# A two-layer diffusion step: one list order through layer 0, and the last output tiles, the norm and the modulation by halves of the tokens

## The chip, the cores and the metric

The kernel runs on one core of a Trainium2 chip, as one program and one launch. The metric is the time of one execution on the device in microseconds (us), the median over runs. The engines are named as in the profile: PE (TensorE matmul), PEld (its weight load), DVE (VectorE), ACT (ScalarE), POOL (GpSimd), SP (SyncE, which issues most DMAs here).

## The reference, cut to what matters

There are 128 prompt tokens and 512 sample tokens of width 1024. The kernel keeps them as 640 columns: two halves of 320, each with 64 prompt and 256 sample tokens. Layer 0 has a convolution branch, layer 1 a state-space branch.

```python
for i in range(DEPTH):                                   # two layers
    hp = rms_norm(yp, norm_g[i]) * (1.0 + sc_p) + sh_p   # shift, scale, gate: silu(cond) @ ada_w
    hs = rms_norm(ys, norm_g[i]) * (1.0 + sc_s) + sh_s
    # layer 0, conformer_branch:
    a, a_gate, z = split(h @ w_in + b_in, 3)             # 3 x 2048 channels
    v = depthwise_conv(a * sigmoid(a_gate), w_dw, b_dw)  # 31 taps; sample tokens in rows of 64
    v = silu(layer_norm(v, ln_g, ln_b))                  # over 2048 channels of a token
    out = (v * silu(z)) @ w_out
    # layer 1, ssd_branch: projection, 5-tap convolution, scan in chunks, norm, w_out
    yp = yp + gt_p * out_p
    ys = ys + gt_s * out_s
```

## The kernel before, in words

Everything lies with channels on the 128 partitions and the 640 tokens along the free axis. A product with a weight tile of 1024 x 128 is made in three passes on PE (high part by high part, high by low, low by high), in two halves of 320 columns: 8 x 3 x 2 = 48 matmuls of 128x320. So each weight tile is loaded (`wf`), rounded by ACT to a high part (`wh`, L477 or L78), and its rest becomes the low part `wl`. In the first part of layer 0 (`split`, L474 to L482) ACT writes minus `wh` into `wl`, and a DMA issued by POOL adds the weight to it from memory. In the rest of layer 0 (`split_w`, L73 to L80) POOL or DVE subtracts.

Layer 0 has 48 such tiles of `w_in`: `a0` to `a15`, `g0` to `g15` (the gate of `a`) and `z0` to `z15`. From an `a` and a `g` tile DVE makes the convolution's input `v` (L529). Of the 31 taps of a channel tile, ACT makes one into an accumulator `cva` in PSUM (L627), DVE adds most of the others there (L635), and `NPOOL[i]` of them are made by ACT (`tp`, L666) and added by POOL to a copy of the sum in SBUF (`cv`, L707). Two accumulators are at work at a time, those of channel tiles `i` and `i + 1`. When `cv[i]` is complete, ACT squares it, and PE sums the tile and its square over the channels (`quarter_sums`, L190: eight matmuls of 160 columns, each of which shows as two in the trace). For tiles 0 to 9 these sums go to spare columns of the PSUM tile of a later `a` product, and DVE adds them to `ssum` in SBUF (L539).

The order of the work on each engine is written out in two ways:

- From the fourth tile of layer 0 (`a1`) to `z6` a list scheduler, the class `Order`, gives it. Chains of steps (Python generators) say which engine a step needs, its duration as planned, what it waits for (`key`, or a free buffer, `get`) and what it frees (`put`). `run` emits the step that can begin first by the plan's clocks; on a tie the lower number of `PRIO0` wins. `PLAN0` is the order of the products on PE. Each engine then works strictly in the order that was emitted; semaphores keep it right whatever the times are.
- From `z7` to layer 1's third tile the code is plain (L742 to L892), in an order that another scheduler makes: the products `z7` to `z15`, the sums of tiles 10 to 15 (into a PSUM tile `pst`), mean and root (L785 to L801), 16 times `normalise` and `gate_z` (L806 to L817), then the output product in three passes over channel tiles m = 0, 1; 2 to 5; 6, 7 (`dense`, L148), where DVE adds each result to the residual `x` (L168) and ACT squares it (L853). Then come the last four blocks of the modulation weights (`ada`), the sum of squares, root and spread (`rps`, `rq`), the modulation to `h_hi` and `h_lo`, and layer 1's first three tiles `dt`, `xs`, `xs`, whose halves are 384 and 256 columns (`ODD`).

From layer 1's fourth tile on a second `Order` with its own priorities plans the rest (`project`, L1006, and so on).

The PSUM tiles: `mm` is two of 2 x 512 columns, `cva` two of 1024. An accumulator is columns 0 to 639 of a `cva` tile.

Of the kernel before, what the change touches and what calls it, by code (L numbers as in the profile page):

```python
# [7 lines left out]
F32 = mybir.dt.float32  # L8
# [29 lines left out]
NCST0 = _n - NCST  # L38


@with_exitstack
def trunk(ctx: ExitStack, tc: tile.TileContext, a: dict):
# [99 lines left out]
    ODD = ((0, 384, 0), (384, NT, 128))  # L142
# [92 lines left out]
    PE, ACT, VE, PO, SP, VL = range(6)  # L235

    class Order:
        def __init__(self, prio):
            self.clock = [0.0] * 5
            self.table = None  # L240
            self.port = 0.0
            self.keys = {}
            self.rings = {}
            self.chains = []
            self.count = 0
            self.prio = prio
            self.same = [-OVER[e_] for e_ in range(5)]

# [46 lines left out]
        def run(self, until=None):  # L295
            while self.chains:
# [4 lines left out]
                for ch in self.chains:  # L301
# [3 lines left out]
                    for n, (eng, dur, fn, table) in enumerate(ways):  # L305
                        shared = eng in (PO, VL)
                        eng = VE if eng == VL else eng
# [96 lines left out]
    with tc.tile_pool(name="l0", bufs=1) as lp:  # L404

        def cs(name, dt=F32):
            return lp.tile([P, NT], dt, tag="cs", bufs=32, name=name)

        ssum = lp.tile([P, 2, QN], F32, name="ssum")
        LAG = 10  # L410
        N_Z = 7

        Z_END = list(range(N_Z, 16))
        order = [32 + j for j in Z_END]

        def z_more(n):
            for _ in range(min(n, len(Z_END))):
                z_tile(Z_END.pop(0))
        ahead = []

        def in_tile(mt):
            while len(ahead) < 2 and order:
                m = order.pop(0)
                ahead.append((m, split_w(a["w_in1"][m], 1024, G)))
            m, (wh, wl) = ahead.pop(0)
            assert m == mt
            ps = mm(f"u{mt}_")
            dense_all(ps, wh, wl, h, [k * 128 for k in range(KD)])
            return ps

# [11 lines left out]
        def rows(t):  # L442
            return t.rearrange("p (r w) -> p r w", w=64)

        sz = [None] * 16

        def z_tile(j):
            ps = in_tile(32 + j)
            sz[j] = cs(f"sz{j}")
            S.activation(out=halves(sz[j]), in_=ps[:, :, 0:HN], func=AF.Silu, bias=c("b_in", 32 + j))  # L450

        def cst_w(name):
            return cs(name)
# [12 lines left out]

        def weights():
            for m in tiles0 + order[:2]:
                yield get("wf")
                wf = gp.tile([P, 1024], F32, tag="wf", bufs=2, name="wf")  # L470
                t = yield op(SP, 0.35, lambda: nc.sync.dma_start(out=wf, in_=a["w_in1"][m]))
                start(split(m, wf), t)

        def split(m, wf):  # L474
            yield get("wh")
            wh = gp.tile([P, 1024], F32R, tag="wh", bufs=3, name="wh")
            t = yield op(ACT, 1.05, lambda: S.copy(out=wh, in_=wf))  # L477
            put("wf", t)
            yield get("wl")
            wl = gp.tile([P, 1024], F32R, tag="wl", bufs=3, name="wl")  # L480
            yield op(ACT, 1.05, lambda: S.activation(out=wl, in_=wh.bitcast(F32), func=AF.Copy, scale=-1.0))  # L481
            t = yield op(PO, 1.1, lambda: G.dma_start(out=wl, in_=a["w_in1"][m], accum_op=ALU.add))  # L482
            t += 4.0
            W0[m] = wh, wl
            post(("w", m), t)
            if m in order[:2]:
                ahead.append((m, W0[m]))

        def product(m, lead=None):
# [3 lines left out]
            if lead is not None:  # L493
                yield op(PE, 1.4, lambda: lead(ps))
            wh, wl = W0[m]
# [12 lines left out]

        def after_g(i, ps, n=None):
# [5 lines left out]
            if n is not None:  # L515
                l, b, ws = rows_[n][0]
                r = ap.tile([P, P], F32, tag="ada_row", bufs=2, name="ada_row")
                t = yield op(ACT, 0.26, lambda: S.copy(out=r, in_=ps[:, 0, HN : HN + 128]))
                rows_[n] = l, b, r
                post(("row", n), t)  # L520
# [3 lines left out]
        def after_a(i, ps, n=None, j=None):  # L524
# [12 lines left out]
            if j is not None:  # L537
                sums = ps[:, :, HN : HN + QN]
# [1306 lines left out]
```

## Time and profile before

| | |
|---|---|
| median of 3 runs | 1101.43 us (1100.14 to 1103.24) |
| the profiled execution's own time | 1099.79 us |
| its span, first to last instruction | 1098.0 us |
| mean granted TensorE clock | 0.989 |
| PE busy | 1055.7 us (96%) |
| DVE busy | 817.2 us (74%) |
| ACT busy | 625.8 us (57%) |
| POOL busy | 467.6 us (43%) |

Busy time is the time in which an engine had an instruction at work; matmuls overlap, so a busy PE can still be one whose clock is halved. In lists of instructions the columns are start and duration in us, engine, line, operation, output<-inputs, shapes, and in brackets the idle time ahead and what ended it. In a table by stretches each engine has its busy time and, in brackets, its instructions.

### The profile page before, as it was taken

Reading aid. Unit: us, or ns where it says so; the run is one execution under the profiler, and the core shown is the slowest. Engines: PE = TensorE matmul, PEld = TensorE weight load, DVE = VectorE, ACT = ScalarE, POOL = GpSimd, SP = SyncE. Lnnn points to the kernel's source line nnn. Section 1 sums busy time; section 2 is a strip of 40 time slices with the busy share of each in tenths; the row PEclk is TensorE's granted clock in tenths of the full one; section 3 lists DMA queues with packets and bytes.
Section 4 is the critical chain, followed back from the end, with each engine's and each line's share of the span. In section 5 each row is a group of like instructions: output and inputs, shape, how many; then the busy total and the mean of one; then the engine's idle time right before and its main releaser. Section 6 shows DMA issues by size and latency. Waiting matters only on the chain.

```text
span 1098.0 us, 19890 instructions
## 1 busy us (share of the span) xinstructions
PE 1055.7 (96%) x7896; PEld 979.0 (89%) x7896; DVE 817.2 (74%) x1155; ACT 625.8 (57%) x1059; POOL 467.6 (43%) x448
## 2 busy tenths in 40 slices
PE   6989999999998999999999999999999999999996
PEld 4889999999988998999899888899889888978896
DVE  2489999999989389413369789988766786767673
ACT  6656777768875366312376657593545473743442
POOL 1128887757998237200000066414551443244313
PEclk9999999999998999999999999999999999999998
DMA  9588788876565111613302463424342414343102
GB/s 361 196 230 204 166 208 203 200 176 145 123 136 114 58 39 41 209 58 118 115 27 91 105 151 104 107 70 125 106 109 84 116 61 113 108 120 94 46 20 96
DMA packets 84526, 135.93 MB, mean 124 GB/s; under 512 B 26705, under 2 KB 49617, under 8 KB 84433
## 3 DMA queue, kind: packets, MB, share of 16 engines
q1 hardware_dynamic: 78240, 113.92, 34.5%
q0 software_dynamic: 5472, 19.93, 10.7%
q8 instruction: 62, 1.02, 0.4%
q10 hardware_dynamic: 720, 0.82, 0.2%
q14 instruction: 32, 0.25, 0.1%
HBM read 129.72 MB, written 4.92 MB: 123 GB/s over the span
## 4 chain that ended last, share of the span: by engine, by line
PE 65%; DVE 19%; ACT 5%; POOL 4%; issue 4%; DMA 2%; SPq 0%; POOLq 0%; DVEq 0%; ACTq 0%
PE pz L1006 8%; PE o L1006 8%; DVE cva L635 7%; PE xs L1006 6%; POOL cv L707 3%; PE o L1515 3%; PE po L1287 2%; PE pst L1224 2%; PE B L1006 2%; PE py L1355 2%; DVE xs L1048 2%; DVE cn L807 2%; PE C L1006 1%; PE o__5617 L148 1%; PE o__5618 L148 1%
## 5 line engine op out<-in xcount | busy, mean ns | idle before, releaser
L635 DVE SCALAR_TENSOR_TENSOR cva<-v,cst,cva 128x540 f32<-128x540 f32 (+12 forms) x359 | 278.0, 821 | 10.2 <-ACT cva L627 5.2
L707 POOL TENSOR_TENSOR cv<-cv,tp 128x490 f32<-128x490 f32 (+5 forms) x121 | 149.7, 1237 | 8.2
L968 ACT CAST wh<-wf 128x1024 fp32r<-128x1024 f32 x53 | 55.5, 1047 | 83.3 <-PE xs L1006 21.1
L666 ACT ACTIVATE tp<-v,cst 128x490 f32<-128x490 f32 (+5 forms) x121 | 82.9, 715 | 31.6 <-POOL cv L707 31.5
L972 DVE TENSOR_TENSOR wl<-wf,wh 128x1024 fp32r<-128x1024 f32 x51 | 67.5, 1323 | 33.3 <-ACT wh L968 32.8
L1006 PE MATMUL o<-yhl,wh 128*128 128x320 f32 x384 | 92.2, 327 | 0.0
L78 ACT CAST wh<-wf 128x1024 fp32r<-128x1024 f32 (+1 forms) x37 | 31.8, 860 | 96.2 <-PE o__5148 L148 38.9
L1006 PE MATMUL pz<-h_hi,wh 128*128 128x384 f32 (+1 forms) x256 | 84.7, 331 | 0.5 <-ACT up L1035 0.5
L1006 PE MATMUL pz<-h_hi,wl 128*128 128x384 f32 (+1 forms) x256 | 79.2, 309 | 0.0
L1006 PE MATMUL pz<-h_lo,wh 128*128 128x384 f32 (+1 forms) x256 | 79.2, 309 | 0.0
L1293 POOL TENSOR_TENSOR y<-y,yo 128x512 f32<-128x512 f32 x32 | 44.6, 1394 | 80.6 <-DVE yo L1291 80.5
L80 DVE TENSOR_TENSOR wl<-wf,wh 128x512 fp32r<-128x512 f32 (+1 forms) x25 | 27.1, 1086 | 68.7 <-ACT wh L78 68.5
L1006 PE MATMUL xs<-h_hi,wh 128*128 128x384 f32 (+1 forms) x224 | 77.5, 346 | 0.0
L1006 PEld LDWEIGHTS o<-yhl,wh 128*128 128x128 f32 x384 | 63.9, 188 | 7.8 <-issue 7.8
L1048 DVE SCALAR_TENSOR_TENSOR xs<-up,cst,xs 128x642 f32<-128x642 f32 x64 | 68.1, 1066 | 2.2 <-ACT xs L1046 0.8
L1006 PE MATMUL xs<-h_hi,wl 128*128 128x384 f32 (+1 forms) x224 | 69.3, 309 | 0.0
L1006 PE MATMUL xs<-h_lo,wh 128*128 128x384 f32 (+1 forms) x224 | 69.2, 309 | 0.0
L1006 PE MATMUL o<-yhl,wl 128*128 128x320 f32 x192 | 59.4, 309 | 0.0
L1168 ACT ACTIVATE gf<-gf,cols 128x128 f32<-128x128 f32 x160 | 49.8, 391 | 16.3 <-DVE gf L1164 16.2
L1162 POOL TENSOR_TENSOR gb<-gb,cols 128x512 f32<-128x512 f32 x20 | 25.5, 1274 | 77.5 <-DMA gb<-acd 77.5
L482 POOL DMA_DIRECT2D wl<-w_in x38 | 33.2, 873 | 53.3 <-ACT wl L481 33.7
L80 POOL TENSOR_TENSOR wl<-wf,wh 128x1024 fp32r<-128x1024 f32 (+1 forms) x12 | 26.4, 2203 | 64.3 <-ACT wh L78 64.3
(764 smaller groups left out, 3491.0 us busy)
## 6 DMA issues: line engine op xcount, KB each, us to landing
wf<-w_in SPq DMA_DIRECT2D x48, 512.0 KB, 3.8
wl<-w_in POOLq DMA_DIRECT2D x38, 512.0 KB, 6.6
wa<-w_ada SPq DMA_DIRECT2D x64, 256.0 KB, 6.5
wf<-w_out SPq DMA_DIRECT2D x24, 512.0 KB, 3.8
wf<-w_xbc SPq DMA_DIRECT2D x24, 512.0 KB, 3.8
gf<-acd SPq DMA_DIRECT2D x40, 256.0 KB, 5.2
wa<-w_ada SPq DMA_DIRECT2D x16, 512.0 KB, 9.9
wf<-w_z SPq DMA_DIRECT2D x16, 512.0 KB, 4.0
```

The source lines that it names most:

```text
L80: sub.tensor_sub(out=wl[:, :n], in0=wf[:, :n], in1=wh[:, :n].bitcast(F32))
L482: t = yield op(PO, 1.1, lambda: G.dma_start(out=wl, in_=a["w_in1"][m], accum_op=ALU.add))
L635: t = yield op(VE, 0.24 + 0.01 * (hi - lo), lambda: V.scalar_tensor_tensor(out=rows64(accs[i], lo, hi), in0=rows64(vs[i], lo + d, hi + d), ...
L666: t = yield op(ACT, 0.72, lambda: S.activation(out=tp[:, :, 0 : hi - lo], in_=rows64(vs[i], lo + d, hi + d), func=AF.Copy, scale=w_dw(i, t ...
L707: t = yield op(PO, 1.12 if i < 14 else 1.3, lambda: G.tensor_add(out=rows64(cv[i], lo, hi), in0=rows64(cv[i], lo, hi), in1=sgs["tp", i, n] ...
L968: S.copy(out=cell["wh"], in_=cell["wf"])
L972: e_.tensor_sub(out=cell["wl"], in0=cell["wf"], in1=cell["wh"].bitcast(F32))
L1006: T.matmul(ps[:, b, at_ : at_ + t1 - t0], lhsT=w_, rhs=t_[:, t0:t1], start=k == 0 and n == 0, stop=k == nk - 1 and n == 2)
L1048: t = yield op(VL, 0.89, lambda: V.scalar_tensor_tensor(out=acc, in0=u[:, d : d + PW], scalar=c("w_c", j * 5 + d), in1=acc, op0=ALU.mult, ...
L1168: t = yield op(ACT, 0.39, lambda: S.activation(out=gv[:, h_, :], in_=gv[:, h_, :], func=AF.Exp, bias=cols1[ch][:, o8 + h_ : o8 + h_ + 1]), ...
L1293: t = yield op(PO, 1.29, lambda: G.tensor_add(out=y, in0=y, in1=yo))
L1515: T.matmul(ps, lhsT=wt, rhs=t_[:, tok], start=k == 0 and n == 0, stop=k == 3 and n == 2)
```

## The change

- `PLAN0` now runs through `z15`, and the list scheduler goes on to the end of layer 1's third tile: statistics, normalisation, output passes, norm, modulation and the three tiles are chains in it. The plain code is gone.
- The weights of the output product and of layer 1's first tiles go through the same chain `split`. Output weights come in 16 tiles of 1024 columns in place of 8 x 512, 8 x 1024 and 8 x 512, and get `wl` by the accumulating DMA; the very first tile and layer 1's three get it by a subtraction on DVE or POOL.
- The sums of all 16 tiles go to columns 640 to 799 of the two `cva` tiles (`whole`), whose columns 0 to 639 are the accumulators, and are added up there by PE; `ssum` in SBUF and its additions are gone, and so is the separate `pst`.
- Mean and root stay in PSUM after they are spread; the four copies to SBUF are gone. The gating product and `y_lo` go to DVE or POOL, whichever the plan finds free first.
- All 16 blocks of modulation weights go ahead of `g` and `z` products (12 before).
- The output tiles m = 6, 7 are made for one half of the tokens, then for the other; residual, squares, root, modulation and layer 1's first three products follow by halves. One of the four weight tiles of that pass lies in buffers of `v`.
- Layer 1 uses halves of 320 everywhere (`EVEN`); steps that read its PSUM tiles are cut accordingly.
- `PRIO0`, `NPOOL` and several planned durations have other values.

The diff, cut to its core:

```diff
+PLAN0 = "a1 g2 g3 a2 g4 a3 g5 a4 g6 a5 a6 g7 g8 z0 a7 a8 g9 g10 a9 a10 g11 g12 a11 z1 a12 g13 a13 z2 z3 z4 g14 g15 a14 z5 a15 z6 z7 z8 z9 z10 z11 z12 z13 z14 z15"
+NPOOL = (11, 8, 15, 11, 6, 10, 12, 5, 3, 9, 2, 2, 5, 8, 7, 6)
...
-        LAG = 10
-        N_Z = 7
...
+            src = [(("w", m), a["w_in1"][m]) for m in tiles0]
+            for pi, nc_ in ((0, 4), (1, 8), (2, 4)):
+                src += [(("out", pi, n), a[f"w_out1_{pi}"][n]) for n in range(nc_)]
+            src += [(("l1", n), w) for n, w in enumerate((a["w_dt"], a["w_xbc"][0], a["w_xbc"][1]))]
...
+                if name[0] == "l1" or name == ("w", tiles0[0]):
+                    t = yield either((VL, 1.23, lambda: V.tensor_sub(out=wl, in0=wf, in1=wh.bitcast(F32))), (PO, 2.44, lambda: G.tensor_sub(out=wl, in0=wf, in1=wh.bitcast(F32))), bias=0.0)
+                    put("wf", t)
+                    post(name, t)
+                    return
+                put("wf", t)
+                yield op(ACT, 1.06, lambda: S.activation(out=wl, in_=wh.bitcast(F32), func=AF.Copy, scale=-1.0))
+                t = yield op(PD, 0.7, lambda: G.dma_start(out=wl, in_=src, accum_op=ALU.add))
+            t += 6.6
+            post(name, t)
...
+            start(add_sums(j), t)
+
+        begun = []
+
+        def add_sums(j):
+            def sums():
+                begun.append(j)
+                for t_, s in ((cv[j], 0), (sgs["sq", j], 1)):
+                    quarter_sums(ssum[s], t_, len(begun) == 1, len(begun) == 16)
+            t = yield op(PE, 0.78, sums)
+            put("tm", t)
+            post(("sums", j), t)
 
...
-                        def sums():
-                            for t_, b in ((cv[j], 0), (sgs["sq", j], 1)):
-                                quarter_sums(ps[:, b, HN : HN + QN], t_, True, True)
-                        t = yield op(PE, 0.78, sums)
-                        put("tm", t)
+            for _ in range(16):
+                put("hT", t)
+            yield from out_pass(0, 0, ("mm", "mm"), 4, 4)
+            yield from out_pass(1, 2, ("cva", "cva", "mm", "mm"), 8, 2)
+            yield from out_halves()
...
-                yield get("cva")
-                accs[i] = cvp.tile([P, 1024], F32, tag="cva", bufs=2, name="cva")[:, 0:NT]
+                yield get(f"cv{i % 2}")
+                accs[i] = whole[i % 2][:, 0:NT]
...
+        def stats():
+            t = yield key(*[("sums", j) for j in range(16)])
+            rq = mr[:, 1]
+            start(means(), t)
+            yield op(ACT, 0.35, lambda: S.activation(out=msq, in_=ssum[0], func=AF.Square, scale=1.0 / 2048))
+            yield op(VE, 0.37, lambda: V.scalar_tensor_tensor(out=rq, in0=ssum[1], scalar=1.0 / 2048, in1=msq, op0=ALU.mult, op1=ALU.subtract))
+            post(("read",), run.clock[VE])
+            yield op(VE, 0.37, lambda: V.scalar_tensor_tensor(out=rq, in0=rq, scalar=0.0, in1=rq, op0=ALU.max, op1=ALU.max))
+            yield op(ACT, 0.45, lambda: S.activation(out=rq, in_=rq, func=AF.Sqrt, bias=epsb), "sqrt")
+            t = yield op(VE, 1.2, lambda: V.reciprocal(out=rq, in_=rq))
+            post(("rq",), t)
+            yield from spread_row(1, rq)
...
+        def spread_row(n, r):
+            yield get("cva")
+            pmr[n] = cvp.tile([P, 1024], F32, tag="cva", bufs=2, name="pmr").rearrange("p (b n) -> p b n", b=2)
+            t = yield op(PE, 1.2, lambda: quarter_spread(pmr[n], r))
+            post(("mu", "rl")[n], t)
...
+        def normalise():
+            yield key("mu", "rl")
+            for i in range(16):
+                yield get("v")
+                t = tmp.tile([P, NT], F32, tag="v", bufs=4, name="cn")
+                yield op(VE, 0.87, lambda: V.tensor_sub(out=halves(t), in0=halves(cv[i]), in1=pmr[0][:, :, 0:HN]))
+                z_ = yield op(VE, 0.87, lambda: V.tensor_mul(out=halves(t), in0=halves(t), in1=pmr[1][:, :, 0:HN]))
+                put("cs", z_)
+                start(gate_z(i, t), z_)
+            put("cva", z_)
+        def gate_z(i, t):
+            yield op(ACT, 0.85, lambda: S.activation(out=t, in_=t, func=AF.Silu, scale=c("ln_g", i), bias=c("ln_b", i)), "silu")
+            yield key(("z", i))
+            z_ = yield either((VL, 0.85, lambda: V.tensor_mul(out=sz[i], in0=t, in1=sz[i])), (PO, 1.4, lambda: G.tensor_mul(out=sz[i], in0=t, in1=sz[i])), bias=0.6)
+            put("v", z_)
...
+            t_ = yield either((VL, 0.85, lambda: V.tensor_sub(out=yl[i], in0=sz[i], in1=yh[i].bitcast(F32))), (PO, 1.4, lambda: G.tensor_sub(out=yl[i], in0=sz[i], in1=yh[i].bitcast(F32))), bias=0.3)
...
+        def out_pass(pi, m0, rings, items, nk):
+            nm = len(rings)
+            pss = []
+            for it in range(items):
+                yield key(("out", pi, it))
+                wh, wl = W0["out", pi, it]
+                ks = range(it * nk, it * nk + nk)
+                for k, j in [(k, j) for k in ks for j in range(nm)] if it < items - 1 else [(k, j) for j in range(nm) for k in ks]:
+                    if it < items - 1 or not j:
+                        yield key(("y", k))
+                    if len(pss) == j:
+                        yield get(rings[j])
+                        pss.append(bank(rings[j], f"o{m0 + j}_"))
+
+                    def step():
+                        dense(pss[j], wh, wl, (k % nk * nm + j) * 128, yh[k], yl[k], k == 0, k == 15)
...
+            for b, tok in enumerate((slice(0, HN), slice(HN, NT))):
+                ks = [k for it in ((0, 1, 2, 3) if b == 0 else (0, 2, 3, 1)) for k in range(4 * it, 4 * it + 4)]
+                every = [(j, k) for k in ks[:12] for j in range(2)] + [(j, k) for j in range(2) for k in ks[12:]]
+                for j, k in every:
...
+        def half_residual(b, m, ps, tok):
+            for cd, sl in SEGS:
+                xv = x[m][:, tok][:, sl]
+                t = yield op(VE, 0.26 + 0.2 * cd, lambda: V.scalar_tensor_tensor(out=xv, in0=ps[:, b, sl], scalar=gain(0, m, cd), in1=xv, op0=ALU.mult, op1=ALU.add))
...
+        def root(b):
+            tok = slice(b * HN, b * HN + HN)
+            rows = slice(64 * b, 64 * b + 64)
+            yield key(("acc", 5), ("o",))
+            t = yield op(PE, 0.2, lambda: sums_x(b, 0, racc[0], tok))
...
+        def modulation(b, ps, tok):
...
+                for cd, sl in SEGS:
+                    z_ = yield op(VE, 0.26 + 0.2 * cd, lambda: V.scalar_tensor_tensor(out=mo[:, sl], in0=x[k][:, tok][:, sl], scalar=gsc[1][:, k, cd : cd + 1], in1=ps[:, b, sl], op0=ALU.mult, op1=ALU.mult))
+                start(split_h(b, k, mo, hi, lo), z_)
...
+            whole += [cvp.tile([P, 1024], F32, tag="cva", bufs=2, name="cva") for _ in range(2)]
+            ssum = [z_[:, NT : NT + QN] for z_ in whole]
...
-        with tc.high_priority(offset=1000):
-            V.tensor_add(out=ssum, in0=ssum, in1=pst[:, :, 0:QN])
...
-        def normalise(i):
-            t = cvp.tile([P, 1024], F32, tag="cva", bufs=2, name="cn")[:, 0:NT]
-            then(V.tensor_sub(out=t, in0=cv[i], in1=mu))
-            then(V.tensor_mul(out=t, in0=t, in1=rl))
-            S.activation(out=t, in_=t, func=AF.Silu, scale=c("ln_g", i), bias=c("ln_b", i))
-            scaled.append(t)
...
-            t = yield from dense_steps(ps, *W[i], h, [k * 128 for k in range(KD)], ODD)
+            t = yield from dense_steps(ps, *W[i], h, [k * 128 for k in range(KD)], EVEN)
```

More of the change, by code (lines that the diff above doesn't have):

```diff
@@ L406, in cs @@
         def cs(name, dt=F32):
-            return lp.tile([P, NT], dt, tag="cs", bufs=32, name=name)
-        ssum = lp.tile([P, 2, QN], F32, name="ssum")
-        LAG = 10
-        N_Z = 7
[L413 to L429, printed above, removed]
+            return lp.tile([P, NT], dt, tag="cs", bufs=33, name=name)
+        mr = lp.tile([P, 2, QN], F32, name="mr")
+        msq = lp.tile([P, QN], F32, name="msq")
         cv = [None] * 16
@@ L469, in weights @@
                 yield get("wf")
                 wf = gp.tile([P, 1024], F32, tag="wf", bufs=2, name="wf")
[L471 to L487, printed above, removed]
+                t = yield op(SP, 0.35, lambda: nc.sync.dma_start(out=wf, in_=w))
@@ L507, in trunk, with row_copy, lead_of, lead @@
         sgs, vs = {}, {}
+        def row_copy(n, ps):
+            l, b = BLOCKS[n]
+            r = ap.tile([P, P], F32, tag="ada_row", bufs=2, name="ada_row")
+            t = yield op(ACT, 0.26, lambda: S.copy(out=r, in_=ps[:, 0, HN : HN + 128]))
+            rows_[n] = l, b, r
+            post(("row", n), t)
+        def lead_of(n):
+            def lead(ps):
+                for k, w in enumerate(rows_[n][0][2]):
+                    for b in range(2):
+                        q = 64 * b + k % 2 * 32
+                        T.matmul(ps[q : q + 32, 0, HN : HN + 128], lhsT=scz[:, k, :], rhs=w[:, b * 128 : b * 128 + 128], start=k < 2, stop=k >= KD - 2)
+            return lead
         def after_g(i, ps, n=None):
@@ L515, in after_g, with after_a @@
             if n is not None:
[L516 to L520, printed above, removed]
+                yield from row_copy(n, ps)
+                t = run.keys["row", n]
             if i != 1:
                 put("mm", t)
-        def after_a(i, ps, n=None, j=None):
+        def after_a(i, ps, n=None):
             yield key(("sg", i))
@@ new lines, in trunk, with spare @@
+        last = {}
+        def spare():
+            for ring in ("mm", "cva"):
+                yield get(ring)
+                last[ring] = bank(ring, "xs")
+            post(("o",), 0.0)
+        def half_residual(b, m, ps, tok):
+            for cd, sl in SEGS:
+                xv = x[m][:, tok][:, sl]
+                t = yield op(VE, 0.26 + 0.2 * cd, lambda: V.scalar_tensor_tensor(out=xv, in0=ps[:, b, sl], scalar=gain(0, m, cd), in1=xv, op0=ALU.mult, op1=ALU.add))
+            post(("half", b, m), t)
+            yield get("tp")
+            sq = last["sq", b, m] = lp.tile([P, 560], F32, tag="tp", bufs=3, name="rms_sq")
+            t = yield op(ACT, 0.47, lambda: S.activation(out=sq[:, 0:HN], in_=x[m][:, tok], func=AF.Square))
+            post(("half_sq", b, m), t)
@@ L711, in begin, with scales @@
+        def scales():
+            for k in range(KD):
+                yield key(("mod", 4 + k))
+                t = yield op(ACT, 0.25, lambda: ada_scale(1, k))
+                post(("gs", k), t)
         def begin():
@@ L885, in trunk @@
[L885 to L891 removed]
+            start(stats(), 0.0)
+            start(normalise(), 0.0)
+            start(scales(), 0.0)
+            start(root(0), 0.0)
+            start(root(1), 0.0)
```

385 lines of the change are left out of this document (202 added, 183 removed).

## The prediction

> **What bounds the kernel.** I read the page first.
>
> ```profile
> span 1098.0 us, 19890 instructions
> ...
> PE 1055.7 (96%) x7896; PEld 979.0 (89%) x7896; DVE 817.2 (74%) x1155; ACT 625.8 (57%) x1059; POOL 467.6 (43%) x448
> ...
> PEclk9999999999998999999999999999999999999998
> ```
>
> PE works 1055.7 of 1098.0 us, so a gain must be idle or slow PE time. The clock row is full but for a few slices. The table by stretches (length, then busy time of PE, PEld, DVE, ACT and POOL, granted clock, DMA share, GB/s) says where PE stands idle:
>
> ```profile
> 57.00:80.00 23.00, 18.62 (x139) 17.70 (x138) 20.07 (x26) 12.01 (x18) 5.50 (x11) 0.93 0.93 264
> 80.00:260.00 180.00, 180.00 (x1550) 177.10 (x1549) 177.77 (x248) 130.85 (x197) 131.04 (x151) 1.00 0.78 189
> 260.00:345.00 85.00, 80.66 (x616) 78.56 (x614) 78.72 (x105) 70.27 (x102) 79.17 (x89) 1.00 0.61 131
> 345.00:436.00 91.00, 84.93 (x614) 81.66 (x615) 69.09 (x78) 49.68 (x69) 45.09 (x29) 0.96 0.17 49
> 436.00:540.00 104.00, 104.00 (x718) 103.50 (x716) 34.04 (x42) 23.60 (x30) 10.04 (x6) 0.98 0.40 125
> 540.00:573.00 33.00, 29.46 (x291) 27.40 (x290) 20.22 (x34) 21.52 (x40) 1.16 (x10) 1.00 0.10 34
> ```
>
> From 57 to 80 it loses 4.4 us, from 80 to 260 nothing, from 260 to 345 4.3, from 345 to 436 6.1, from 436 to 540 nothing, from 540 to 573 3.5. DVE is as full as PE up to 345 (177.8 of 180, 78.7 of 85), then no more: the convolution binds DVE and PE together, what follows binds PE alone. PE's list of waits names the gaps, and PE's order in time the one at the start:
>
> ```profile
> PE u__4136 L157 <- ACT sz L545: 4.3, 1, 4.3
> PE o__4900 L148 <- DVE wl L80: 2.6, 1, 2.6
> PE u__3759 L501 <- ACT sg L513: 2.4, 1, 2.4
> ...
> PE ada L122 <- DVE mod L129: 1.1, 2, 0.9
> ...
> PE u__3108 L122 <- ACT ada_row L518: 0.8, 1, 0.8
> PE dt L148 <- DVE h_lo L219: 0.8, 1, 0.8
> PE dt L148 <- ACT h_hi L214: 0.8, 1, 0.8
> PE pz L1006 <- ACT up L1035: 0.5, 1, 0.5
> ```
>
> ```profile
> 70.82 0.64 PE L501 MATMUL u__775<-h_hi,wl 128*128 128x320 f32 x1 [4.08 <-DMA wl<-w_in]
> ```
>
> The two longest waits cost more than their length, as the chain of work in order of time and a narrow stretch show (the stretch: length, PE's busy time, granted clock, DMA share, GB/s):
>
> ```profile
> 322.07 7.04 PE u__3849 L501 x48
> ...
> 348.37 9.90 PE u__4136 L157 x48
> ...
> 435.68 1.14 PE o__4900 L148 x4
> 436.82 1.07 PE o__4901 L148 x4
> 437.89 1.60 PE o__4900 L148 x6
> ```
>
> ```profile
> 437.00:438.00 1.00, 1.00 (x6) 0.50 0.52 178
> ```
>
> A product of 48 matmuls takes 7.04 us; `u__4136` (`z7`), after the wait of 4.3, takes 9.90: 2.86 more, at half the clock. After the wait of 2.6 the first 4, 4 and 6 matmuls take 1.14, 1.07 and 1.60 us in place of 0.59, 0.59 and 0.88 (7.04 / 48 each): 1.75 more. After 2.4 us at `u__3759` the clock stays full (80.66 of 85 at clock 1.00).
>
> The Trainium skill, "TensorE: Matmul & The Clock Gate", Part 1, halves the clock after an idle window of about 3.4 us. The trace has the half clock after 2.56 us too. By the rule alone the 1.75 us would not belong to that wait, and the sum below would come out 1.75 higher.
>
> **The change part by part.** PE's own work stays: the same 48 matmuls a tile, 384 + 256 columns become 320 + 320, four blocks of modulation products move from 540 to 300 or so, the sums move. So I count PE's lost time, against the profiled execution's 1099.8 us, which is 1.6 under the median.
>
> *The wait at `z7`.* It is behind ACT, which came late to two evacuations. In the new order `z6` to `z15` follow `a15` in the same plan as ACT's work, so I take the whole: -4.3 - 2.9 = -7.2. If another evacuation comes late, it returns (rival 3).
>
> *The wait at the first output tiles* (`o__4900`), for a low part that DVE makes between normalisations: now a DMA makes it. -2.6 - 1.75 = -4.3. What takes its place:
>
> ```profile
> L968 ACT CAST wh<-wf 128x1024 fp32r<-128x1024 f32 x53 | 55.5, 1047 | 83.3 <-PE xs L1006 21.1
> ...
> L80 DVE TENSOR_TENSOR wl<-wf,wh 128x512 fp32r<-128x512 f32 (+1 forms) x25 | 27.1, 1086 | 68.7 <-ACT wh L78 68.5
> ...
> L482 POOL DMA_DIRECT2D wl<-w_in x38 | 33.2, 873 | 53.3 <-ACT wl L481 33.7
> ...
> wl<-w_in POOLq DMA_DIRECT2D x38, 512.0 KB, 6.6
> ```
>
> One weight tile lasts PE 7.04 us, and with three buffers a tile may take two of these, 14.1, from free buffer to use: ACT's copy 1.05, POOL's issue of 0.87 and 6.6 to land are 8.5, covered. If that cover went, 16 tiles would each show the excess. DVE loses 25 subtractions (27.1 us), POOL gains 16 issues (14 us) in a stretch where it works 10 of 104 us. On SP 24 loads become 16, and the loads of four modulation blocks move ahead of the last `g` tiles, where the transfers have room (share 0.61 from 260 to 345); if they came late there, `z2` to `g15` would wait on PE at their lead, up to a landing's time each.
>
> *The waits at `g15` and `a12`* (2.4 and 0.8) are drift between plan and chip, which a new plan can have again: half, -1.6 (0 to -3.2). *The start* (4.08) waits for a landing DMA, as it will after; ACT's new priorities may send it earlier: -0.5 (0 to -1.3).
>
> *Sums into the accumulators' tiles.* DVE loses ten additions:
>
> ```profile
> L539 DVE TENSOR_TENSOR ssum<-ssum,u__2007 x1: 480/480/480, 183.3 to 183.3; 128x320 f32<-128x320 f32 x1
> ...
> L539 DVE TENSOR_TENSOR ssum<-ssum,u__3849 x1: 481/481/481, 332.8 to 332.8; 128x320 f32<-128x320 f32 x1
> ```
>
> 4.8 us, counted at nothing: they shorten the convolution, whose end the ten `z` products (70 us) cover. But PE now writes into a PSUM tile that DVE's taps read and write. If the program lets the two take turns there, each of 14 sums (tiles 0 to 13; for the last two no taps are left) ties the queues together: PE waits for the tap at hand, DVE's next tap for PE.
>
> ```profile
> L635 DVE SCALAR_TENSOR_TENSOR cva<-v,cst,cva x359: 746/827/880, 60.3 to 362.1; 128x550 f32<-128x550 f32 x19, 128x580 f32<-128x580 f32 x18, 128x540 f32<-128x540 f32 x17, 128x560 f32<-128x560 f32 x17
> ```
>
> ```profile
> 266.39 0.48 PE L190 MATMUL u__3108<-cv,ones 128*32 128x160 f32 x8
> 266.68 0.45 PE L190 MATMUL u__3108<-sq,ones 128*32 128x160 f32 x8
> 266.95 1.06 PE L584 MATMUL u__3205<-wa,scz 128*32 128x128 f32 x32
> ```
>
> No row of before shows the two in one PSUM tile. Bounds for one sum: 0, if they go on side by side; a tap of 0.82 plus both groups, 0.29 + 0.45 = 0.74, hence 1.56, if everything stands. Taps mostly alternate between the two tiles. Ends the tap at hand in the second tile, the first group has run beneath it and the second runs under the next tap: nothing. Ends it in the first, the next tap waits 0.74. The mean is about 0.4, with taps that do not alternate 0.5. Since both queues are full and in fixed order, what DVE loses PE loses at the next sum, and all that stands behind these taps (`v`, hence the `mm` buffer of the next `a`) comes later too. 14 x 0.5 = +7.0 (0 to +21.8).
>
> The Trainium skill, "PSUM — Partial Sum Buffer", section "PSUM bank collisions raise a hardware error", says that software must keep two engines apart by bank and quadrant even where their columns differ. Accumulator columns from 512 on and the sums would then share a bank. By it 0 drops out, and the sum cannot reach the second rival's time; no row here shows it.
>
> *Normalisation* reads mean and root from PSUM and shares its work with POOL.
>
> ```profile
> 385.00:437.00 52.00, 49.31 (x326) 48.18 (x325) 47.88 (x50) 34.14 (x49) 30.02 (x16) 0.99 0.12 38
> ```
>
> It takes 52 us now, DVE full. Begun at about 375 it ends by 427 even at that pace. PE reaches the output product at about 419: `a15` ends at 329.1 (322.07 + 7.04), plus `z5` 7.0, four blocks of 1.06, the sums' 7, less the 1.6, plus ten products. It needs the last `y` three quarters into the first pass of 28 us, at 440: covered by 13 us, +0. If it were not, PE would wait for each tile at DVE's pace of 3.2 us.
>
> *Halves.* Before, PE loses 3.5 us from 540 to 573, with four modulation blocks of 1.06 as filling. After, the first half's chain runs beside the second half's 14 us of products. Its pieces:
>
> ```profile
> 541.93 0.74 ACT L853 ACTIVATE rms_sq<-x 128x640 f32<-128x640 f32 x1
> ...
> 563.07 1.28 ACT L1714 ACT_TABLE_LOAD   x1 [0.92 <-issue]
> ...
> 570.17 1.05 ACT L968 CAST wh<-wf 128x1024 fp32r<-128x1024 f32 x1 [5.61 <-PE dt L148]
> ```
>
> ```profile
> 544.17 1.14 DVE L195 RECIPROCAL rq<-rq 128x160 f32<-128x160 f32 x1
> ...
> 571.26 1.23 DVE L972 TENSOR_TENSOR wl<-wf,wh 128x1024 fp32r<-128x1024 f32 x1 [8.26 <-ACT wh L968]
> ```
>
> Square 0.74 (half a tile: less), root's table 1.28 and root, reciprocal 1.14, then residual, spread, modulation and split, estimated from these at 0.5 to 0.8 each: about 8.5 us, under 14. The second half's chain runs beside the first half's 10.6 us of layer 1: 2 us in hand, but DVE needs an estimated 1.4 us a step (two passes of 0.5 to 0.7) against PE's 1.32, so I leave 2.0. At layer 1's start the freed weight buffer sets the pace: ACT's copy 1.05, DVE's subtraction 1.23, after `dt` ends; `dt` now ends 0.9 before the last product, 1.8 before, so the 0.5 of `pz` becomes 1.4. Together 3.4 in place of 3.5: 0 (-1.5 to +6).
>
> *The tail's fixed order* replaces an order that was also fixed; new small waits +1.0 (0 to +4). Layer 1's plan is made anew with the same durations: 0 (2 either way).
>
> Sum: -7.2 - 4.3 - 1.6 - 0.5 + 7.0 + 0 + 1.0 = -5.6, so 1094.2 for the profiled execution, **1095.8** for the median.
>
> **The rivals.** Each is the sum with one term changed.
>
> 1. *The forecast*: sums at 0.3 to 0.8 us each: 1090 to 1100.
> 2. *The sums are free*, because taps and sums go side by side or the plan's order already fits: -12.6, 1089. For it: PE waits for nothing from 80 to 260 now. Against: DVE and PE are both full there, so any tie is felt.
> 3. *A gap comes back*: at one place, an evacuation by ACT or a low part landing late, PE stands still over 2.5 us and then runs at half clock, as at `z7`: -5.6 + 7.2 = +1.6, 1103. For it: ACT was late at `g15` and `z7`, both in planned stretches. Against: those rows are of one stretch, where POOL was full (79.2 of 85).
> 4. *The sums are dear*, and the kernel is slower: each stops PE and DVE for a whole tap and both groups, 14 x 1.56 = 21.8: -12.6 + 21.8 = +9.2, 1110.6. It is slower than before by over 0.3% from 1.14 us a sum on. For it: both queues are full and in order. Against: two accumulators alternate.
>
> **How the numbers follow.** Chances: forecast 0.42, free sums 0.27, gap 0.13, dear sums 0.15, something else 0.03. A change of 0.3% (3.3 us) is about what a measurement of this kernel can tell from none. Faster (under 1098.1): three quarters of the forecast, 0.32, and the free sums, with some of the rest, 0.28: 0.60. Within: the other quarter less a little and most of the gap: 0.20. Slower: 0.15 and 0.05 of the rest: 0.20. The range leaves a tenth on each side: 1085, the free sums with every small term at its good end, to 1108, short of the dear sums' full price.
>
> **What the profile would show.** No wait of over 1 us at `z7`'s or the first output tiles' place, and a clock row without the two dips between 345 and 440. PE's waits for DVE at the sums' line (the 160-column matmuls), about 14, each under 1 us; DVE's taps waiting for PE about as often. From 80 to 260 PE under 180 of 180. Around the halves, waits of 2 us in all. Wrong would be: no such waits and a gain beyond 12 us; waits of 1.2 us and more at every sum; a low part of the output weights as the releaser of PE; or one wait over 2.5 us with half clock behind it.

## The result, and the profile after

The changed kernel takes 1106.1 us (median; 1103.38 to 1108.58) against 1101.07 before in the same series: 1.0047 times as long, 95% interval 1.0031 to 1.0063, so slower. Forecast were 1095.8. The profiled execution of after is the longest of its runs (own time 1108.58, that of before 1099.79). The page of after:

```profile
span 1106.8 us, 19938 instructions
...
PE 1061.7 (96%) x7904; PEld 979.2 (88%) x7904; DVE 804.6 (73%) x1181; ACT 650.8 (59%) x1070; POOL 448.5 (41%) x447
...
PEclk9989999999999999999899999999999999999998
```

The stretches that the prediction showed of before, now of after:

```profile
57.00:80.00 23.00, 18.66 (x144) 17.81 (x146) 20.14 (x28) 10.96 (x17) 5.35 (x8) 0.85 0.97 273
80.00:260.00 180.00, 174.69 (x1518) 166.85 (x1511) 161.03 (x218) 135.41 (x206) 145.67 (x160) 1.00 0.78 189
260.00:345.00 85.00, 83.49 (x733) 79.94 (x732) 75.01 (x106) 55.06 (x78) 47.08 (x58) 1.00 0.73 167
345.00:436.00 91.00, 90.31 (x646) 88.38 (x646) 78.56 (x105) 69.25 (x88) 36.03 (x41) 1.00 0.65 139
436.00:540.00 104.00, 103.67 (x707) 101.52 (x707) 22.04 (x35) 40.51 (x47) 12.19 (x14) 1.00 0.62 138
540.00:573.00 33.00, 31.12 (x185) 28.70 (x185) 22.48 (x68) 15.92 (x37) 1.16 (x10) 0.90 0.11 34
```

The two gaps with half clock between 345 and 440 are gone: 90.31 of 91 and 103.67 of 104, clock 1.00. New are a loss of 5.3 us from 80 to 260, where PE was full before, and a stretch at clock 0.90 from 540 to 573. PE's waits (total, times, longest):

```profile
...
PE u__765 L499 <- DMA wl<-w_in: 4.3, 1, 4.3
PE cva L195 <- DVE cva L648: 3.0, 6, 1.0
PE o__5673 L853 <- DVE modo L936: 2.1, 5, 0.6
PE o L1109 <- ACT zs L1228: 1.9, 1, 1.9
PE cva L195 <- POOL seam L707: 1.6, 3, 0.6
PE rms L1511 <- ACT ysq L1501: 1.5, 1, 1.5
...
PE pz L1109 <- ACT up L1138: 1.5, 1, 1.5
PE pst L1326 <- DVE yo L1393: 1.4, 1, 1.4
PE cva L195 <- ACT tp L678: 1.3, 1, 1.3
PE cva L195 <- POOL cv L719: 1.3, 1, 1.3
```

The first row is the wait at the start, which before has too. L195 are the sums, L853 the products of the last two output tiles, L936 the modulation; `o`, `rms`, `pst` belong to layer 1.

Three rows of PE's order in time cut both programs into the same four stages: the second planned product, the first output product, and `pz`, layer 1's fourth tile. (In after four modulation blocks stand ahead of that second product, so its row is theirs.) Before, then after:

```profile
79.20 0.31 PE L501 MATMUL u__863<-h_hi,wh 128*128 128x320 f32 x1
...
421.16 0.46 PE L148 MATMUL o__4900<-y_hi,wh 128*128 128x320 f32 x2
...
572.37 0.45 PE L1006 MATMUL pz<-h_hi,wh 128*128 128x384 f32 x1 [0.47 <-ACT up L1035]
```

```profile
79.56 0.64 PE L519 MATMUL u__860<-wa,scz 128*32 128x128 f32 x16
...
428.21 0.45 PE L153 MATMUL o__4930<-y_hi,wh 128*128 128x320 f32 x2
...
575.28 0.41 PE L1109 MATMUL pz<-h_hi,wh 128*128 128x320 f32 x1 [1.48 <-ACT up L1138]
```

The last stage ends with the span. The same rows cut the experiments (times in us; ratio to before in each kernel's own series):

| kernel | median | ratio to before, 95% | start | list to `z15` | output, norm, three tiles | layer 1 |
|---|---|---|---|---|---|---|
| before | 1101.07 | | 79.2 | 342.0 | 151.2 | 525.6 |
| after | 1106.10 | 1.0047 (1.0031 to 1.0063) | 79.6 | 348.6 | 147.1 | 531.5 |
| norm apart | 1102.01 | 1.0011 (0.9999 to 1.0023) | 79.3 | 348.6 | 141.3 | 529.3 |
| sums elsewhere | 1100.32 | 0.9995 (0.9985 to 1.0006) | 81.1 | 343.0 | 144.4 | 529.3 |
| sums late | 1099.02 | 0.9984 (0.9970 to 0.9998) | 79.7 | 340.2 | 145.9 | 531.3 |
| layer 1 in 384 + 256 | 1101.95 | 1.0007 (0.9994 to 1.0019) | 81.3 | 348.6 | 147.1 | 526.5 |
| before, layer 1 in 320 | 1106.78 | 1.0050 (1.0031 to 1.0070) | 79.2 | 343.4 | 151.3 | 531.2 |
| layer 1's order | 1101.38 | 1.0015 (1.0004 to 1.0026) | 79.2 | 348.4 | 144.4 | 527.4 |
| planned as 384 + 256 | 1101.89 | 1.0014 (1.0001 to 1.0026) | 78.3 | 348.5 | 144.4 | 527.4 |
| silu in two | 1108.67 | 1.0067 (1.0047 to 1.0087) | 81.2 | 348.5 | 147.1 | 534.8 |
| norm apart, 384 + 256 | 1098.53 | 0.9981 (0.9968 to 0.9994) | 79.7 | 348.6 | 141.3 | 527.6 |
| all three | 1089.85 | 0.9904 (0.9884 to 0.9924) | 81.1 | 340.2 | 141.3 | 525.7 |

Before to after by stages: +0.4, +6.6, -4.1, +5.9, together the 8.8 us between the two spans. An edit changes its own stage and leaves the others, apart from some 3 us at the start and half clocks that come and go (last section): with the same order of work layer 1 takes 531.5 or 531.3 in after and sums late, which have a half clock there, and 529.3 in norm apart and sums elsewhere, which have none. Differences below are between medians of different series; with intervals of 1 to 2 us on either side of each ratio, a difference under some 2 us cannot be told from none.

### The profile page after: what moved, and what is told of

The parts are those of the page before. It is cut to its first block, busy times and chain, and to the rows that moved or that the text cites. A ratio compares the mean times of both kernels' runs of the same rounds, so it can differ in the third digit from the quotient of the medians.

```text
span 1106.8 us, 19938 instructions
## 1 busy us (share of the span) xinstructions
PE 1061.7 (96%) x7904; PEld 979.2 (88%) x7904; DVE 804.6 (73%) x1181; ACT 650.8 (59%) x1070; POOL 448.5 (41%) x447
## 5 line engine op out<-in xcount | busy, mean ns | idle before, releaser
L648 DVE SCALAR_TENSOR_TENSOR cva<-v,cst,cva 128x610 f32<-128x610 f32 (+13 forms) x360 | 277.7, 822 | 26.3 <-PE cva L195 13.3
L719 POOL TENSOR_TENSOR cv<-cv,tp 128x490 f32<-128x490 f32 (+6 forms) x120 | 151.6, 1264 | 8.2
L472 ACT CAST wh<-wf 128x1024 fp32r<-128x1024 f32 x63 | 65.8, 1044 | 91.0 <-PE o__5231 L153 29.8
L1071 ACT CAST wh<-wf 128x1024 fp32r<-128x1024 f32 x53 | 55.5, 1048 | 87.1 <-PE o L1109 32.7
L678 ACT ACTIVATE tp<-v,cst 128x490 f32<-128x490 f32 (+6 forms) x120 | 83.0, 722 | 32.7 <-POOL cv L719 32.1
L1109 PE MATMUL pz<-h_hi,wh 128*128 128x320 f32 x256 | 85.5, 334 | 1.5 <-ACT up L1138 1.5
L1109 PE MATMUL pz<-h_hi,wl 128*128 128x320 f32 x256 | 79.1, 309 | 0.0
L1109 PE MATMUL pz<-h_lo,wh 128*128 128x320 f32 x256 | 79.0, 309 | 0.0
L1109 PE MATMUL xs<-h_hi,wh 128*128 128x320 f32 x224 | 77.2, 344 | 0.0
L1109 PE MATMUL xs<-h_hi,wl 128*128 128x320 f32 x224 | 69.2, 309 | 0.0
L1109 PE MATMUL xs<-h_lo,wh 128*128 128x320 f32 x224 | 69.1, 309 | 0.0
```

The lines of the kernel that those rows point to most:

```text
L648: t = yield op(VE, 0.24 + 0.01 * (hi - lo), lambda: V.scalar_tensor_tensor(out=rows64(accs[i], lo, hi), in0=rows64(vs[i], lo + d, hi + d), ...
L678: t = yield op(ACT, 0.72, lambda: S.activation(out=tp[:, :, 0 : hi - lo], in_=rows64(vs[i], lo + d, hi + d), func=AF.Copy, scale=w_dw(i, t ...
L719: t = yield op(PO, 1.28 + 0.0175 * (hi - lo - 49), lambda: G.tensor_add(out=rows64(cv[i], lo, hi), in0=rows64(cv[i], lo, hi), in1=sgs["tp" ...
L1071: S.copy(out=cell["wh"], in_=cell["wf"])
L1109: T.matmul(ps[:, b, at_ : at_ + t1 - t0], lhsT=w_, rhs=t_[:, t0:t1], start=k == 0 and n == 0, stop=k == nk - 1 and n == 2)
```

## The experiments

My theory A: the gains came as forecast, and three costs outweigh them: the sums in the accumulators' tiles, the halves of the norm, and layer 1's list.

**The norm apart.** In after, the spread root of the first half lies in bank 0 of the tile `o__5673`, while PE writes the second half's products into bank 1 of the same tile. PE and DVE in after, in time (in brackets the wait and its releaser):

```profile
537.67 0.67 DVE L936 SCALAR_TENSOR_TENSOR modo<-x,gsc,o__5673 128x64 f32<-128x64 f32 x2 [2.59 <-PE o__5673 L853]
...
538.39 0.41 PE L853 MATMUL o__5673<-y_hi,wh 128*128 128x320 f32 x1 [0.33 <-DVE modo L936]
...
540.01 0.28 DVE L936 SCALAR_TENSOR_TENSOR modo<-x,gsc,o__5673 128x64 f32<-128x64 f32 x1 [0.54 <-PE o__5673 L853]
...
540.94 0.41 PE L853 MATMUL o__5673<-y_hi,wh 128*128 128x320 f32 x1 [0.52 <-DVE modo L936]
...
543.15 0.28 DVE L936 SCALAR_TENSOR_TENSOR modo<-x,gsc,o__5673 128x64 f32<-128x64 f32 x1 [0.80 <-PE o__5673 L853]
...
543.49 0.76 PE L853 MATMUL o__5673<-y_hi,w_o 128*128 128x320 f32 x2 [0.37 <-DVE modo L936]
```

They take turns, step by step. The edit:

```diff
-            ps = last["o"][0]
+            ps = last["o"][0] if b else last["cva"]
...
-            start(modulation(b, ps, tok), t)
...
+            t = yield op(ACT, 0.47, lambda: S.copy(out=rs[:, tok], in_=ps[:, b, 0:HN]))
+            start(modulation(b, rs, tok), t)
```

> The changed kernel, but the spread root of the first half of the tokens goes to a free `cva` tile, and ACT copies each half's spread root (0.47 us as planned) to SBUF, where the modulation reads it. So DVE's modulation of the first half no longer reads the PSUM tile into which PE writes the second half's products. Theory A (three sources, of which this tie is one): from 520 to 573 the products lose about 11 us now, 3.4 of it at half clock after a row of waits of 0.3 to 0.6; these waits and the half clock go, two copies of about 0.5 come in: 4 to 7 us less than the changed kernel's 1106.1, so 1099 to 1102. Rival A1 (PE waits there for the chain itself - residual, root, modulation are simply late - whatever tile they lie in): within 1.5 us of 1106.1, the same waits with other names. Rival A2 (the half clock at 543 is chance): waits go, half clock stays, 2 to 3 us less.

Measured 1102.0, 4.1 less than after; the stage goes from 147.1 to 141.3. PE's waits from 520 to 573, and the stretch, of this kernel:

```profile
PE pz L1114 <- ACT up L1143: 1.4, 1, 1.4
PE o__5675 L874 <- DVE x L890: 0.3, 1, 0.3
```

```profile
540.00:573.00 33.00, 31.28 (x209) 29.53 (x208) 25.43 (x71) 21.35 (x48) 1.16 (x10) 1.00 0.15 47
```

The five waits for the modulation are gone, so A1 falls: it was the tile, not a late chain. The half clock went with them, against A2; but it is chance in so far as three kernels with the tie run this stage at full clock, in 144.4 (the table). After and two others with the tie have 6.8 us at half clock there, and take 147.1. So 3.1 us are turns (144.4 - 141.3), and 2.7 (147.1 - 144.4) the half clock.

**The sums elsewhere.** One sum in after, on PE and on DVE:

```profile
190.19 0.48 PE L195 MATMUL cva<-cv,ones 128*32 128x160 f32 x8 [1.27 <-POOL cv L719]
190.46 0.48 PE L195 MATMUL cva<-sq,ones 128*32 128x160 f32 x8
```

```profile
187.93 1.55 DVE L648 SCALAR_TENSOR_TENSOR cva<-v,cst,cva 128x510 f32<-128x510 f32 x2 [2.02 <-ACT cva L640]
190.99 2.38 DVE L648 SCALAR_TENSOR_TENSOR cva<-v,cst,cva 128x520 f32<-128x520 f32 x3 [1.51 <-PE cva L195]
```

DVE's second tap ends at 189.48, PE's sum comes at 190.19, and DVE's next tap stands 1.51 us until the sum is through. The sum came late because it had itself waited 1.27 us for POOL's last addition to `cv`: the shared tile hands POOL's lateness on to DVE. In all, DVE's waits in after:

```profile
DVE cva L648 <- PE cva L195: 13.3, 15, 1.5
```

```diff
+                if j < 13:
+                    for t_ in (cv[j], sgs["sq", j]):
+                        quarter_sums(cur[0][:, cur[1], HN : HN + QN], t_, True, True)
+                    return
```

> The changed kernel, but the sums of channel tiles 0 to 12 are written to spare columns of the product tile (the bank that PE is not adding into at that time) in place of the accumulators' tiles; PE's matmuls are the same in number, shape and place. It leaves out: those 13 sums never reach the statistics, and they overwrite rows of the modulation results. So it is a price and no remedy. Theory A (a sum and DVE's taps take turns in one PSUM tile): the waits at the sums' line (6.4 us in all) and DVE's 13.3 us for the sums go, a sum costs about 0.75 in place of 1.34: 6 to 10 us less than 1106.1, so 1096 to 1100. Rival A3 (the sums cost PE what they cost before, and the new cost lies elsewhere: DVE is not the bound any more because its additions are gone): within 2 us of 1106.1, PE waits for `v` or buffers instead.

The sums of tiles 0 to 12 never reach the statistics in this kernel, so it prices them and is no remedy. Measured 1100.3, 5.8 less than after (just short of the expected 6); the stage goes from 348.6 to 343.0. DVE's waits for the sums from 80 to 430, and the first stretch:

```profile
DVE cva L654 <- PE cva L195: 1.4, 2, 0.7
```

```profile
80.00:260.00 180.00, 178.25 (x1548) 170.16 (x1548) 166.10 (x225) 136.37 (x207) 147.63 (x161) 1.00 0.80 195
```

Same matmuls at the same places, and 3.6 of the 5.3 us are back. So A3 falls: the tie costs. 5.8 over 13 sums is 0.45 each.

**The sums late**, a remedy that computes everything: no sum before the convolution of tile 14 ends, then all into that tile's free accumulator.

```diff
-            yield key(("cv", j))
+            yield key(("cv", j), ("cv", 14))
...
-            ssum = [z_[:, NT : NT + QN] for z_ in whole]
+            ssum = [whole[0][:, 512 : 512 + QN], whole[0][:, 0:QN]]
```

> The changed kernel, but all 16 sums wait until the convolution of channel tile 14 is complete, and both go into that tile's accumulator, which no tap uses any more. All is computed. Theory A (the tie of sums and taps in one PSUM tile costs, not the sums): as with the sums in spare columns of the product tiles, 5 to 7 us less than 1106.1, so 1099 to 1101; DVE's 13.3 us of waits for the sums go, and normalisation still ends before the output product needs it. Rival A6 (what went when the sums were moved aside was only half the matter: 16 squares and sums in one heap make the statistics late): a wait at the first output tiles of 2 us or more, 1102 to 1107.

Measured 1099.0, 7.1 less than after; the stage takes 340.2. The sums' line, with its first and last start, and the stretch of the first output tiles:

```profile
L195 PE MATMUL cva<-cv,ones x128: 299/299/323, 355.3 to 378.4; 128*32 128x160 f32 x128
```

```profile
436.00:520.00 84.00, 84.00 (x578) 83.35 (x577) 11.79 (x21) 29.19 (x33) 11.29 (x13) 1.00 0.69 151
```

All sixteen lie between 355 and 379, PE has nothing to wait for at the first output tiles (84.00 busy of 84), and A6 falls. What the sums take of PE can be counted from its rows, as the time between the product matmuls on either side beyond 0.147 us a matmul: 21.5 us in after (1.34 each), 14.3 in the kernel with the sums elsewhere (0.89), 11.4 here (0.71), where the sixteen interrupt the products only nine times.

**Layer 1 in 384 + 256, and before with layer 1 in 320.** One gives after the former halves of layer 1, the other gives before the new ones.

```diff
+    ODD = ((0, 384, 0), (384, NT, 64))
...
-            t = yield from dense_steps(ps, *W[i], h, [k * 128 for k in range(KD)], EVEN)
+            t = yield from dense_steps(ps, *W[i], h, [k * 128 for k in range(KD)], ODD)
```

> The changed kernel, but layer 1's products from its fourth tile on are again made in halves of 384 and 256 columns, with the evacuations and the silu cut as before the change. Layer 0 and the first three tiles of layer 1 stay changed. Theory A (layer 1's list came out worse with the 320 + 320 halves): layer 1 goes back by 2 to 6 us, so 1100 to 1104, and layer 1's length by the profile from 531.5 toward 525.6. Rival A4 (the 5.9 us of layer 1's length are the profiled run's own, or come from the state in which layer 0 leaves the engines): within 1.5 us of 1106.1.

> The kernel before, with the layer 1 part of the change alone: all of layer 1's products in halves of 320, its first three tiles included, the evacuations and the silu cut as after the change. Layer 0 is as before. Theory A: 2 to 6 us slower than before, 1103 to 1107. Rival A4 (layer 1's list is no worse): within 1.5 us of 1101.

Measured 1101.95, 4.2 less than after, and 1106.8, 6.0 more than before in its series (1100.8); layer 1 takes 526.5 and 531.2. A4 falls, and from both sides: with the halves of 320 layer 1 costs some 4 to 6 us more, whatever layer 0 does.

**Layer 1's order.** Is it the matmuls of 320 columns, or the list? Here the halves stay 320, and only the scheduler's durations and the silu's steps are those of before.

```diff
-                    t = yield op(PE, 3 * ((t1 - t0) / 2400 + 0.0135), step)
+                    t = yield op(PE, 3 * (((384, 256)[b] if banks is EVEN else t1 - t0) / 2400 + 0.0135), step)
...
-            t = yield op(ACT, 0.79, lambda: S.activation(out=zh, in_=ps[:, :, 0:HN], func=AF.Silu), "silu")
+            yield op(ACT, 0.6, lambda: S.activation(out=zh[:, :, 64:HN], in_=ps[:, :, 64:HN], func=AF.Silu), "silu")
+            t = yield op(ACT, 0.27, lambda: S.activation(out=zh[:, :, 0:64], in_=ps[:, :, 0:64], func=AF.Silu), "silu")
```

> The changed kernel with 320 + 320 columns in layer 1, but the list scheduler is told the durations of 384 and 256 columns for these halves, and the silu is two steps as before the change; so the list comes out in the order that the halves of 384 and 256 get. Theory A1 (the order of layer 1's list is what costs): as the kernel with halves of 384 and 256, 1100 to 1103.5. Rival A7 (the halves of 320 themselves cost, in matmuls or evacuations): within 1.5 us of 1106.1.

Measured 1101.4, 4.7 less than after (3.5 by the two ratios to before); layer 1 takes 527.4. A7 falls: the order costs, not the halves. But the order is not the one expected, that of the halves of 384 and 256; it is a third one (below). The two halves of this edit alone (first hunk: planned as 384 + 256; second: silu in two):

> The changed kernel with one half of the order remedy of layer 1: the silu of a gate tile is two steps again (128 x 512, then 128 x 128 columns), the planned durations of the matmuls stay those of 320 columns. The list with both halves of the remedy gained 4.7 us. If the silu in one step spoils the order: 3 to 5 us less than 1106.1, 1101 to 1103. If the planned matmul steps do: within 1.5 us of 1106.1. If either edit gives the scheduler a luckier list: both single edits gain.

> The changed kernel with the other half of the order remedy: matmuls of 320 columns planned with the durations of 384 and 256, the silu in one step. If the planned matmul steps spoil the order: 1101 to 1103. If the silu does: within 1.5 us of 1106.1. If only both together bring back the old list: neither single edit gains.

Planned as 384 + 256: 1101.9, 4.2 less than after. Silu in two alone: 1108.7, 2.6 more, which none of the three cases had. So the planned durations of the matmuls make the difference. PE's rows from `pz` on, without their times, show which orders these are. The three kernels in 384 + 256 have before's order, in 525.7 to 527.6 us. Before in 320 has after's, in 531.2. Layer 1's order and planned as 384 + 256 share a third, all but a few rows, in 527.4. Silu in two has a fourth, in 534.8, the slowest in the profile, though its interval overlaps after's.

**Together.** Norm apart and 384 + 256, then the late sums as well:

> The changed kernel with two remedies together: the norm's spread root in another PSUM tile with SBUF copies, and layer 1 in halves of 384 and 256. If the two costs are separate (theory A): 1106.1 - 4.1 - 4.2 = 1097.8, so 1096.5 to 1099.5. If they overlap, as would be if both gains were the half clock that comes in some executions after the norm: 1100 to 1102.

> The changed kernel with all three: the norm apart, layer 1 in halves of 384 and 256, and the sums after the convolution of tile 14. All is computed. Theory A: 1106.1 - 4.1 - 4.2 - 5.8 = 1092.0, so 1090 to 1094.5, which would be 0.8% faster than before. If the three costs overlap: 1096 or more.

Measured 1098.5, 7.6 less than after (4.1 + 4.2 = 8.3 if they add), and 1089.85, 16.2 less (with 7.1 for the late sums 15.4), just under the expected 1090 to 1094.5: within the noise the costs add. All three together beat before too, 0.9904 times its time, interval 0.9884 to 0.9924. Its page:

```profile
span 1088.2 us, 19945 instructions
...
PE 1055.7 (97%) x7904; PEld 976.1 (90%) x7904; DVE 797.0 (73%) x1185; ACT 648.8 (60%) x1084; POOL 441.8 (41%) x445
...
PEclk9989999999999999999999999999999999999998
```

## Why the prediction was wrong

It said faster; the kernel is slower. By stages, with the four moved blocks (4.2) counted where they went:

| stage | forecast | profiled |
|---|---|---|
| start | -0.5 | +0.4 |
| list to `z15` | -7.2 - 1.6 + 7.0 + 4.2 = +2.4 | +6.6 |
| output, norm, three tiles | -4.3 - 4.2 + 0 + 1.0 = -7.5 | -4.1 |
| layer 1 | 0 | +5.9 |
| together | -5.6 | +8.8 |

- *The waits at `z7` and at the first output tiles*: right. No such wait is left, the clock row has no dips from 345 to 440, and no low part of the output weights releases PE. (The chain put at 8.5 us leaves out ACT's second copy, that of minus `wh`, 1.06; 9.6 is still under the 14.1 that cover it.) Without the three costs, that is in the kernel with all three edits, 11.4 us are gained on before in its series; the prediction's terms without the sums are -12.6.
- *Sums into the accumulators' tiles, +7.0*: mechanism and size right. "PE's waits for DVE at the sums' line, about 14, each under 1 us; DVE's taps waiting for PE about as often": eleven waits, 7.2 us; the six for DVE are 1.0 at most, the longest, 1.3, is for POOL or ACT; and DVE's 15. The edits give 5.8 for 13 sums and 7.1 for all. It is no case of the dear sums: 0.45 us each, far from 1.14.
- *The rest of the list*: with the late sums the stage is 1.8 under before (340.2), where the terms without the sums gave -4.6. Counted from PE's rows as above, before and with the late sums: between products with nothing else in between 9.4 and 3.9 us, so -5.5 where -7.2 was forecast for `z7`, since other small breaks remain; the sums 14.5 (3.2 of it the waits at `g15` and `a12`) and 11.4, so -3.1 where -1.6 was forecast; the modulation blocks 13.4 and 20.2, so +6.8 where 4.2 was. A block takes 1.2, not 1.06, in the list, and one brought a wait of its own:

```profile
PE u__2128 L499 <- ACT sz L553: 1.4, 1, 1.4
```

- *"Halves ... 0 (-1.5 to +6)"*: the first term that failed. The sum had the first half's chain beside the second half's products, and no wait between the two. But the root is spread into the tile that these products fill, and each modulation step stops them. 3.1 us of turns and, in the profiled run, 2.7 of half clock; 4.1 by the medians. Untied, the stage is 9.9 under before (141.3), better than the forecast of -7.5. The rule of turns that the prediction feared for the sums it did not look for here.
- *"Layer 1's plan is made anew with the same durations: 0 (2 either way)"*: the second, and about as large. It was put at nothing without a look at the durations, and they are not the same: the planned step goes by the columns, so 0.52 and 0.36 us became 0.44 and 0.44, and the list came out in another order. It costs 4.2 to 4.7 by the medians, 6.0 when brought into before. Of the 5.9 in the profiled run some 2.2 are a half clock behind the wait of 1.9 at `o`, since the same order takes 529.3 without it:

```profile
759.00:762.00 3.00, 3.00 (x11) 2.48 (x10) 1.78 (x5) 0.83 (x1) 1.04 (x1) 0.50 0.00 0
```

That leaves 3.7 for the order itself. Of the waits in layer 1, after has 1.9 (`o`), 1.5 (`rms`) and 1.4 (`pst`); before has

```profile
PE po L1287 <- DVE gf L1346: 1.0, 1, 1.0
...
PE rms L1409 <- DVE ysq L1399: 0.6, 1, 0.6
```

These waits are 3.2 us longer, most of the 3.7. Which step of the new order makes them stays open.

- *The rivals*: the number lies between the third rival's 1103 and the dear sums' 1110.6, for the reasons of neither. That it also lies within 1085 to 1108 is luck: no term of the sum held the tie of the halves or the new order at its size. Of the third rival the half clock came true, without its long wait. And that the clock stayed full after 2.4 us at `u__3759`, as read from before, was luck too (last section).

## What to carry to other kernels

A term set to zero needs the same look as a disputed one: for every operation that moves, ask which tile it now shares with a neighbour's running work, and go by the whole tile, not by its banks or columns. When a list scheduler is fed other durations, its whole order is new: that is a change in itself, of either sign, and is costed as one. If several edits come as one, cut the program at a few rows that both versions have; the stages then tell which edit to undo.

## What the runs showed of the hardware

The clock halved without a long idle. Four stretches of 3.41 us of after, around the norm:

```profile
536.84:540.25 3.41, 3.08 (x20) 2.64 (x18) 2.04 (x5) 1.36 (x3) 0.00 (x0) 1.00 0.27 107
540.25:543.66 3.41, 2.19 (x12) 1.50 (x11) 2.17 (x8) 2.49 (x5) 0.00 (x0) 1.00 0.49 154
543.66:547.07 3.41, 2.83 (x10) 2.43 (x11) 1.08 (x3) 0.93 (x3) 0.00 (x0) 0.50 0.00 0
547.07:550.48 3.41, 3.41 (x14) 3.41 (x14) 2.40 (x5) 0.47 (x1) 0.00 (x0) 0.50 0.16 19
```

They are cut so that a border falls on the change of the clock. In the second PE was busy for 2.19 of 3.41 us, with no wait longer than 0.52 (at 540.94, above), and it ran at half clock for the next 6.8. The clock's changes in this trace, at 76.04, 543.67, 550.50, 758.71 and 762.12, lie 137, 2, 61 and 1 times 3.413 us apart: stretches of that length run on through the whole program. Three of the five waits, 1.21 us, fall into the second stretch shown. The kernel with layer 1's order has the same five waits and no half clock:

```profile
PE o__5673 L853 <- DVE modo L936: 2.1, 5, 0.6
```

```profile
540.00:573.00 33.00, 29.63 (x192) 27.36 (x193) 23.59 (x68) 18.83 (x43) 1.16 (x10) 1.00 0.11 33
```

There two of the waits fall into 539.18 to 542.59 and two into 542.59 to 546.00 (PE busy for 2.57 and 2.46), by its own changes of the clock. So it depends on where the waits fall in time, and the same program can differ by it. Layer 0 is the same in before and in before with layer 1 in 320, and in both PE waits 2.4 us at `u__3759`, to the same time; one stays at full clock (the row of 260 to 345 in the prediction has 1.00), the other runs at 0.50. Before, then the other, with a stretch of that length behind the wait:

```profile
314.76 0.41 PE L501 MATMUL u__3759<-h_hi,wh 128*128 128x320 f32 x1 [2.42 <-ACT sg L513]
```

```profile
314.76 0.64 PE L501 MATMUL u__3759<-h_hi,wh 128*128 128x320 f32 x1 [2.44 <-ACT sg L513]
```

```profile
314.56:317.97 3.41, 3.21 (x12) 3.21 (x13) 1.28 (x2) 3.38 (x5) 3.25 (x4) 0.50 0.80 160
```

PE's busy share alone does not decide, though. The kernel with the sums elsewhere has such a stretch with 2.14 us busy, and the clock stays full in it and behind it; what else counts stays open:

```profile
537.99:541.40 3.41, 2.14 (x12) 1.62 (x12) 1.82 (x6) 2.47 (x5) 0.00 (x0) 1.00 0.07 26
```

The Trainium skill, "TensorE: Matmul & The Clock Gate", Part 1, has the clock go by a free-running window of 3413 ns and halve after an idle one. The length agrees with the 6.8 us here, two windows. That the window must be idle does not agree: 64% busy was too little in after.

Turns in a PSUM tile went by the tile. The Trainium skill, "PSUM — Partial Sum Buffer", section "PSUM bank collisions raise a hardware error", asks for guards by bank and quadrant. The halves of `o__5673` lay in two banks, and the program's waits still tied them. They were free of each other once the root was spread into another tile and copied to SBUF, which the experiment did together.
